# Keeping the w_out result in PSUM for its norm, moving the per-layer products, and eight conditioning columns beside w_out

## The chip, the cores and the metric

The kernel runs on one core of a Trainium2 chip. The metric is the device time of one execution in microseconds, taken as the median of several runs of the same program. A core has five engines that run side by side: TensorE (matrix products, PE in the profile, its weight loads PEld), VectorE (DVE), ScalarE (ACT), GpSimd (POOL) and SyncE (SP), whose queue issues nearly all loads. Each engine works through its own instructions in order, and waits on semaphores for the others.

## What is computed

The input is one sequence of 256 positions with 1024 channels. Two blocks follow each other. The first one is, cut to what matters here:

```
mix = concat(rwkv7(z_rw), nsa(z_nsa), s5(z_s5)) @ w_out      # z = rms_norm(h) @ w_in
h = h + rms_norm(mix, post_mix_norm)
f = conv_ffn(rms_norm(h, pre_ffn_norm), w_up, conv_w, conv_b, w_down)
h = h + rms_norm(f, post_ffn_norm)
e = rms_norm(p @ w_ple, ple_norm)                            # the per-layer vector
h = h + sigmoid(h @ w_ple_gate) * e
```

The second block has a pooling mixer, a feed-forward layer, dilated attention, and a last feed-forward layer. Each of its norms is modulated by columns of `silu(c) @ ada_w + ada_b`: 112 columns of 128 channels, each the product of a 1024-long vector with 128 rows of a matrix. Everything is float32 to the accuracy of the reference.

## The kernel before, in words

The sequence stays transposed on the chip: `xT` is 8 tiles of 128 channels by 256 positions. A weight comes as a 512 KB load on SP's queue into a `raw` tile; ScalarE casts it to a rounded part `wr` (L213), VectorE subtracts to get the remainder `wl` (L214), the input is split in the same way into `R` and `L` (L281 and L282, or L284 and L285 with modulation), and each 128 x 128 step is three matrix products: `R` by `wr` (L224), `L` by `wr` (L225), `R` by `wl` (L226). All other products go through one helper (L241).

A norm works as follows. ScalarE squares each of 8 tiles (L249), TensorE sums the squares over channels with a vector of ones (L241, `st<-ones,sq`), VectorE makes mean plus epsilon (`rv`, L269), GpSimd takes the power -1/2 (`rr`, L271), TensorE spreads the factors over all partitions (`st<-cst,rr`), and VectorE multiplies.

The order of each engine's instructions comes from a scheduler that simulates the program as it is written; `high_priority`, `issue_after`, `behind` (a floor under the simulated start of a piece) and `manual_schedule` (an order written by hand for one engine) change it. It is fixed when the program is built.

The stage that the change touches first is the end of the mixers. `products` runs the w_out steps for eight output tiles, held in two PSUM tiles of tag `acc` and two of tag `ms`. Beside them the tail of the RWKV mixer runs: L720 centres the heads, L721 and L722 square and scale them on ScalarE, L1093 sums, L737 takes the power, L1117 spreads it, L742 and L743 finish, and a split feeds the last w_out steps. L756 then copies each result tile, scaled by the norm's gain, into the SBUF tile `F`, and L249 squares it. `post_add` multiplies `F` by the factors (L1248), adds it to `xT` (L1250), and squares and sums the new `xT` for the norm ahead of the feed-forward layer. Then `ada_setup` loads c into `cond` and takes its silu (L1194, L1195), `ada_rows(ROWS[0])` computes one group of four conditioning columns on TensorE (`acc<-adw,ccol`), `norm_split` makes the feed-forward input (L296, L281, L282), `ple_vec` makes the per-layer vector from `pT` and two `w_ple` loads (L1365 and a sum over squares that GpSimd adds in pairs, L253), and `ffn_up` starts.

The conditioning columns come in two ways: singly on VectorE (`ada`, a load and L1208, a multiplication with sum), or in groups of four on TensorE, `ROWS` of them at five places: (1, 2, 0, 0, 2). The last place is the end of the second block's first feed-forward layer, right before `attention_layer`. There, `norm_split` runs twice on the same factors, into `R`, `L` for the queries and into `raw_x` for keys and values; `bt` tiles (L1524) hold the distances scaled by the heads' slopes.

## Time and profile before

| | |
|---|---|
| median of 3 runs | 1255.55 us (1253.08 to 1264.51) |
| the profiled execution | 1257.43 us |
| its span on the core | 1255.6 us |
| mean granted TensorE clock | 0.967 of full speed |

All rows further down come from the profiled execution; times in them count from the start of its span. "Idle before" in a row, in brackets, is how long the engine stood and what ended it. A matmul's own duration is longer than the distance to the next one, since matmuls are pipelined; where a price per row is wanted, the distance of starts counts. The granted clock is 1.00 at 2.4 GHz and 0.50 at 1.2 GHz.

### The profile page before, as it was taken

How to read it: one execution, taken by the hardware profiler on the slowest of the kernel's cores; microseconds unless marked ns; L12 is line 12 of the kernel's file. 1: busy time of each engine (PE TensorE's matmuls, PEld its weight loads, DVE VectorE, ACT ScalarE, POOL GpSimd, SP SyncE). 2: the span in 40 equal slices, each digit the busy share in tenths (PEclk: the TensorE clock that was granted, in tenths of full speed). 3: DMA queues.
4: the chain of work that ended last, by engine and by line, in shares of the span. 5: the costliest groups of instructions: out<-in, count | busy, mean ns of one | idle time of the engine just before them, and what ended most of it. 6: DMA issues, size and time to landing. Idle time of an engine off the chain costs nothing. (4 is left out here: it accounts for less than half of the span.)

```text
span 1255.6 us, 26442 instructions
## 1 busy us (share of the span) xinstructions
PE 1184.4 (94%) x10664; PEld 1116.8 (89%) x10664; DVE 934.8 (74%) x1839; ACT 680.5 (54%) x1197; POOL 95.8 (8%) x121
## 2 busy tenths in 40 slices
PE   5998999899999998899999988999999999999996
PEld 5985777899999988889999987999999989999996
DVE  7899856389999767979998756756675756987653
ACT  7632644366665535556565445545655565666541
POOL 0022200020000102220000010000000002000010
PEclk9998989799999988999999997999999999999998
DMA  8521302377667873666887785665464624666651
GB/s 286 159 87 51 103 27 77 123 255 252 236 235 261 316 272 112 230 205 250 285 301 249 265 296 192 225 218 201 169 217 168 211 93 153 220 250 219 184 185 34
DMA packets 75707, 247.19 MB, mean 197 GB/s; under 512 B 8256, under 2 KB 15680, under 8 KB 75584
## 3 DMA queue, kind: packets, MB, share of 16 engines
q1 hardware_dynamic: 75296, 244.72, 55.8%
q8 instruction: 83, 1.36, 0.4%
q10 hardware_dynamic: 288, 0.79, 0.2%
q14 instruction: 40, 0.33, 0.1%
HBM read 244.42 MB, written 1.05 MB: 195 GB/s over the span
## 5 line engine op out<-in xcount | busy, mean ns | idle before, releaser
L214 DVE TENSOR_TENSOR wl<-raw,wr 128x1024 fp32r<-128x1024 f32 (+3 forms) x340 | 400.8, 1182 | 128.8 <-ACT wr L213 128.0
L213 ACT CAST wr<-raw 128x1024 fp32r<-128x1024 f32 (+3 forms) x340 | 343.0, 1014 | 266.1 <-PE acc L225 210.8
L224 PE MATMUL acc<-R,wr 128*128 128x256 f32 x1424 | 400.2, 282 | 5.5 <-ACT wr L213 5.2
L226 PE MATMUL acc<-R,wl 128*128 128x256 f32 x1424 | 399.9, 281 | 3.9 <-DVE wl L214 3.7
L225 PE MATMUL acc<-L,wr 128*128 128x256 f32 x1424 | 399.5, 281 | 0.0
L224 PEld LDWEIGHTS acc<-R,wr 128*128 128x128 f32 x1424 | 270.3, 190 | 9.8 <-ACT wr L213 5.5
L226 PEld LDWEIGHTS acc<-R,wl 128*128 128x128 f32 x1424 | 271.2, 191 | 7.6 <-DVE wl L214 5.0
L225 PEld LDWEIGHTS acc<-L,wr 128*128 128x128 f32 x1424 | 270.3, 190 | 1.8 <-issue 1.5
L224 PE MATMUL acc<-aR,wr 128*128 128x256 f32 x608 | 168.7, 281 | 7.2 <-ACT aR L281 6.4
L226 PE MATMUL acc<-aR,wl 128*128 128x256 f32 x608 | 169.0, 280 | 2.4 <-DVE wl L214 2.4
L225 PE MATMUL acc<-aL,wr 128*128 128x256 f32 x608 | 168.6, 279 | 0.1
L1208 DVE SCALAR_TENSOR_TENSOR adw<-adw,cond 128x1024 f32<-128x1024 f32 x92 | 113.0, 1232 | 43.9 <-DMA adw<-in_ada_dram 43.5
L224 PEld LDWEIGHTS acc<-aR,wr 128*128 128x128 f32 x608 | 115.1, 191 | 7.8 <-ACT aR L281 6.8
L226 PEld LDWEIGHTS acc<-aR,wl 128*128 128x128 f32 x608 | 115.3, 190 | 3.7 <-DVE wl L214 3.7
L225 PEld LDWEIGHTS acc<-aL,wr 128*128 128x128 f32 x608 | 115.2, 190 | 0.5 <-DVE aL L282 0.3
L253 POOL TENSOR_TENSOR sq<-sq,sq 128x256 f32<-128x256 f32 x42 | 46.4, 1104 | 867.3 <-ACT sq L249 702.2
L224 PE MATMUL acc<-raw_x,wr 128*128 128x256 f32 (+1 forms) x320 | 92.1, 288 | 1.4 <-ACT wr L213 1.1
L225 PE MATMUL acc<-raw_x,wr 128*128 128x256 f32 (+1 forms) x320 | 91.5, 286 | 1.4 <-DVE raw_x L318 1.3
L226 PE MATMUL acc<-raw_x,wl 128*128 128x256 f32 (+1 forms) x320 | 91.6, 287 | 0.8 <-DVE wl L214 0.8
L241 PE MATMUL acc<-wr,raw_x 128*128 128x256 f32 x384 | 69.0, 281 | 0.0
L225 PEld LDWEIGHTS acc<-raw_x,wr 128*128 128x128 f32 x320 | 61.6, 193 | 2.6 <-DVE raw_x L318 2.1
L226 PEld LDWEIGHTS acc<-raw_x,wl 128*128 128x128 f32 x320 | 61.3, 192 | 2.3 <-issue 1.4
(473 smaller groups left out, 1805.8 us busy)
## 6 DMA issues: line engine op xcount, KB each, us to landing
adw<-in_ada_dram SPq DMA_DIRECT2D x92, 512.0 KB, 5.6
raw<-in_ffn_w_up_dram SPq DMA_DIRECT2D x88, 512.0 KB, 4.3
raw<-in_w_up_dram SPq DMA_DIRECT2D x44, 512.0 KB, 3.3
raw<-in_ffn_w_down_dram SPq DMA_DIRECT2D x32, 512.0 KB, 4.1
raw<-in_attn_w_q_dram SPq DMA_DIRECT2D x24, 512.0 KB, 5.7
raw<-in_w_k_dram SPq DMA_DIRECT2D x24, 512.0 KB, 3.4
raw<-in_w_v_dram SPq DMA_DIRECT2D x24, 512.0 KB, 4.1
adw<-in_ada_r_dram SPq DMA_DIRECT2D x20, 512.0 KB, 5.9
```

Of the source, the lines that this page charges most:

```text
L213: nc.scalar.copy(wr, raw)
L214: nc.vector.tensor_sub(wl, raw, wr[:].bitcast(F32))
L224: mm(out, wr, xr, start=start, stop=False)
L225: mm(out, wr, xl, start=False, stop=False)
L226: self.last_mm = mm(out, wl, xr, start=False, stop=stop).ins
L241: self.nc.tensor.matmul(out, lhsT, rhs, start=start, stop=stop)
L253: nc.gpsimd.tensor_tensor(sq, sq, self.sqsum, op=ALU.add)
L1208: nc.vector.scalar_tensor_tensor(w, w, 1.0, self.cond, op0=ALU.mult, op1=ALU.mult, accum_out=self.mod[:, i:i + 1])
```

## The change

The result tiles of w_out stay in their PSUM tiles. A new `mix_add` takes the factors into SBUF (`keep_r`, `rbq`) and multiplies straight from PSUM, gain and factors in one instruction, before it adds to `xT`. `ple_vec` becomes three parts: its loads and its eight products now stand in `mix_add`, its sums and factors inside the first feed-forward step. In the mixers a second silu(c), `KC`, is made, and eight single columns (`MIXC`) are multiplied on VectorE beside w_out, from loads in the mixers' `raw` buffers. The row groups on TensorE go from (1, 2, 0, 0, 2) to (0, 2, 0, 0, 1). Weight casts and remainders made ahead get floors, and so do the `bt` copies and the silu of `cond`. PSUM pools are closed by hand so that the mixers' tiles live on.

```diff
 UPA = 1
+
+MIXC = 8
 MSB = 3
 ADRB = 6
-ROWS = (1,2,0,0,2)
+ROWS = (0,2,0,0,1)
 ZSB = 2
...
         self.since += 1
-        with self.behind(self.hold if self.hold and self.since > NH else self.floor):
+        hold = self.hold if self.hold and self.since > NH else None
+        with self.behind(hold or self.floor[:1]):
             nc.scalar.copy(wr, raw)
+        with self.behind(hold or self.floor):
             nc.vector.tensor_sub(wl, raw, wr[:].bitcast(F32))
...
         sq = self.tmp([128, T], "sq", bufs=3)
-        nc.scalar.activation(sq, x, AF.Square)
+        self.last_sq = nc.scalar.activation(sq, x, AF.Square).ins
         first = n - 2 if pre else 0
         if pre and k < n - 1:
             if k:
                 nc.gpsimd.tensor_tensor(sq, sq, self.sqsum, op=ALU.add)
             self.sqsum = sq
-        def sums():
+        def sums(st=st):
             for h in range(2):
                 self.mm(st[:, h:h + 1], sq[:, h * 128:(h + 1) * 128], self.ones1,
                         start=(k == first and h == 0), stop=(k == n - 1 and h == 1))
-        if later and k == n - 1:
+        if later and k > n - 1 - later and k >= first:
             return sums
...
             v = self.tmp([128, 2], "rv")
-            nc.vector.tensor_scalar(v, st, 1.0 / D, EPS, op0=ALU.mult, op1=ALU.add)
+            self.last_rv = nc.vector.tensor_scalar(v, st, 1.0 / D, EPS, op0=ALU.mult, op1=ALU.add).ins
             r = self.tmp([128, 2], "rr") if r is None else r
...
                     nc.vector.tensor_tensor(Oc[:, j], Oc[:, j], bon[:, j], op=ALU.add)
-                    self.split(Oc[:, j], self.R[:, j], self.L[:, j])
+                    done = self.split(Oc[:, j], self.R[:, j], self.L[:, j])
             k5 = [weights(4 * i, 4, 5, 1) for i in range(2)]
         for w in k4 + k5:
             early(w, self.last_bc)
+        cond = self.mxt([128, D], "KC")
+        nc.sync.dma_start(cond, self.a["c"].to_broadcast([128, D]))
+        nc.scalar.activation(cond, cond, AF.Silu)
+        for i in self.ada_todo[:MIXC]:
+            w = self.rawload(self.a["ada"][i], [128, D])
+            with self.behind(done):
+                nc.vector.scalar_tensor_tensor(w, w, 1.0, cond, op0=ALU.mult, op1=ALU.mult, accum_out=self.mod[:, i:i + 1])
+        nc.vector.tensor_tensor(self.mod[:, 0:MIXC], self.mod[:, 0:MIXC], self.vcol("ada_b_2", 0, MIXC), op=ALU.add)
+        self.ada_todo = self.ada_todo[MIXC:]
         self.dump("o_rw", Oc)
-        F = self.mxt([128, KB, T], "z9")
         st = self.psum("st", 1)
         for m in range(KB):
             if m % 2 == 0:
                 products(c[m // 2], m)
                 products(c[m // 2], m + 1)
-            nc.scalar.activation(F[:, m], out(m), AF.Identity, scale=self.vcol("post_mix_norm", m))
             self.sq_stat(st, out(m), m, pre=False)
-        return self.post_add(F, self.rstd(st[:, 0:2]), True)
+        self.mix_z = out
+        return st
+
+    def mix_add(self, st):
+
+        nc, tc = self.nc, self.tc
+        load, tile, end = self.ple_vec()
+        load()
+        self.keep_r(self.rstd(st[:, 0:2]))
+        sx = self.psum("ms", MSB)
+        with tc.manual_schedule(engines={mybir.EngineType.DVE}):
+            for k in range(KB):
+                y = self.tmp([128, T], "ny", bufs=3)
+                nc.vector.scalar_tensor_tensor(y, self.mix_z(k), self.vcol("post_mix_norm", k), self.rbq, op0=ALU.mult, op1=ALU.mult)
+                x = nc.vector.tensor_tensor(self.xT[:, k], self.xT[:, k], y, op=ALU.add)
+                self.sq_stat(sx, self.xT[:, k], k, pre=False)
+        rb = self.rstd(sx[:, 0:2])
+        self.floor = self.last_sq, self.last_rv
+        for m in range(KB):
+            tile(m)
+        return rb, end
     def nsa_cmp(self):
...
         nc.sync.dma_start(self.cond, a["c"].to_broadcast([128, D]))
-        nc.scalar.activation(self.cond, self.cond, AF.Silu)
+        with self.behind():
+            nc.scalar.activation(self.cond, self.cond, AF.Silu)
     def ada(self, n):
...
         self.ada_rows(ROWS[1])
-        self.post_add(F, self.rstd(st[:, 0:2]), False)
-
-    def post_add(self, F, rb, stat):
+        self.post_add(F, self.rstd(st[:, 0:2]))
+
+    def post_add(self, F, rb):
         nc = self.nc
-        st = self.psum("acc", self.nacc) if stat else None
         with self.tc.manual_schedule(engines={mybir.EngineType.DVE}):
             for k in range(KB + 1):
                 if k < KB:
                     nc.vector.tensor_tensor(F[:, k], F[:, k], rb, op=ALU.mult)
-                if stat and k < KB:
+                if k:
+                    hold = self.split(self.xT[:, k - 1], self.R[:, k - 1], self.L[:, k - 1])
+                if k < KB:
                     nc.vector.tensor_tensor(self.xT[:, k], self.xT[:, k], F[:, k], op=ALU.add)
-                    self.sq_stat(st, self.xT[:, k], k, pre=False)
-                elif not stat:
-                    if k:
-                        hold = self.split(self.xT[:, k - 1], self.R[:, k - 1], self.L[:, k - 1])
-                    if k < KB:
-                        nc.vector.tensor_tensor(self.xT[:, k], self.xT[:, k], F[:, k], op=ALU.add)
-        if not stat:
-            self.keep_free(hold)
-        return st
+        self.keep_free(hold)
     def addg(self, W, R, L, g, kb, hook=None, perm=False, ahead=False):
...
         pT = self.fp.tile([128, 2, T], F32, name="pT", tag="pT", bufs=1)
-        nc.scalar.dma_start(pT, a["p"].rearrange("p (k t) -> p k t", k=2))
-        st = self.psum("st", 1)
-        for c in range(2):
-            w = self.rawload(a["w_ple"][c].rearrange("p (m k f) -> p m k f", m=4, k=2), [128, 4, 2, 128])
-            for i in range(4):
-                m = 4 * c + i
-                pz = self.psum("acc", self.nacc)
-                for k in range(2):
-                    self.mm(pz[:, 0:T], w[:, i, k], pT[:, k], start=(k == 0), stop=(k == 1))
-                nc.scalar.activation(E[:, m], pz[:, 0:T], AF.Identity, scale=self.vcol("ple_norm", m))
-                self.sq_stat(st, pz[:, 0:T], m)
-        rb = self.rstd(st[:, 0:2])
-        for m in range(KB):
-            nc.vector.tensor_tensor(E[:, m], E[:, m], rb, op=ALU.mult)
+        w, st, pz = [], [], []
+
+        def load():
+            nc.sync.dma_start(pT, a["p"].rearrange("p (k t) -> p k t", k=2))
+            for c in range(2):
+                w.append(self.rawload(a["w_ple"][c].rearrange("p (m k f) -> p m k f", m=4, k=2), [128, 4, 2, 128]))
+
+        def tile(m):
+            if m % 2 == 0:
+                pz.append(self.psum("mx" if m < 4 else "acc", 2))
+                for i in range(2):
+                    for k in range(2):
+                        self.mm(pz[-1][:, i * T:(i + 1) * T], w[m // 4][:, m % 4 + i, k], pT[:, k], start=(k == 0), stop=(k == 1))
+            z = pz[-1][:, m % 2 * T:(m % 2 + 1) * T]
+            nc.scalar.activation(E[:, m], z, AF.Identity, scale=self.vcol("ple_norm", m))
+            sums = self.sq_stat(None, z, m, later=2)
+            if sums:
+                st.append(sums)
+
+        def end():
+            s = self.psum("acc", self.nacc)
+            for sums in st:
+                sums(s)
+            rb = self.rstd(s[:, 0:2])
+            for m in range(KB):
+                nc.vector.tensor_tensor(E[:, m], E[:, m], rb, op=ALU.mult)
+        return load, tile, end
     def ple_gate(self, hook):
...
             for r, c in enumerate((slice(0, 256), slice(256, 384), slice(384, 512))):
-                nc.scalar.activation(b_[:, :, c], self.dt[:, :, c], AF.Copy, scale=8.0 * float(DIL_SLOPES[r, 2 * m + hf]))
+                with self.behind():
+                    nc.scalar.activation(b_[:, :, c], self.dt[:, :, c], AF.Copy, scale=8.0 * float(DIL_SLOPES[r, 2 * m + hf]))
             bt.append(b_)
...
     psum = lambda name: tc.tile_pool(name=name, bufs=1, space=PSUM, reuse_waits="tile")
-    with tc.tile_pool(name="wpm", bufs=1, reuse_waits="tile") as n.wp, psum("psm") as n.ps:
+    mixp, ffp = ExitStack(), ExitStack()
+    n.ps = mixp.enter_context(psum("psm"))
+    n.mixp = mixp
+    with tc.tile_pool(name="wpm", bufs=1, reuse_waits="tile") as n.wp:
         n.nraw, n.nw, n.nacc = RAWM, WM, 2
         n.setup()
         st = n.first()
-        n.dump("x1", n.xT)
-        rb = n.rstd(st[:, 0:2])
     n.wp = ctx.enter_context(tc.tile_pool(name="wp", bufs=1, reuse_waits="tile"))
     n.nraw, n.nw, n.nacc = RAWB, WB, ACCB
     rt = ctx.enter_context(tc.tile_pool(name="rt", bufs=1, reuse_waits="tile"))
     n.skip(rt, SKIP_R)
     n.rawt = rt.tile([128, KB, 2, T + 64], F32R, name="raw_x")
     n.cdp = ctx.enter_context(tc.tile_pool(name="cdp", bufs=1, reuse_waits="tile"))
-    with tc.tile_pool(name="fp", bufs=1, reuse_waits="tile") as n.fp, psum("psf") as n.ps:
+    with tc.tile_pool(name="fp", bufs=1, reuse_waits="tile") as n.fp:
         n.tp = n.fp
-        n.ada_setup()
-        n.ada_rows(ROWS[0])
         n.aR = n.fp.tile([128, FT, T], F32R, name="aR")
         n.aL = n.fp.tile([128, FT, T], F32R, name="aL")
+        rb, end = n.mix_add(st)
         n.norm_split(n.xT, rb, n.vcol("pre_ffn_norm", 0, 8), n.R, n.L)
-        n.ple_vec()
-        n.ffn_up(a["w_up"], lambda m: n.ada(ADA[1]), True, "conv_w", "conv_b")
+        n.ada_setup()
+        mixp.close()
+        n.ps = ffp.enter_context(psum("psf"))
+        n.ffn_up(a["w_up"], lambda m: n.ada(ADA[1]) if m else end(), True, "conv_w", "conv_b")
         n.post(a["w_down"], n.aR, n.aL, n.vcol("post_ffn_norm", 0, 8), FT, lambda m: n.ada(ADA[2]))
         n.second_ahead()
         st = n.ple_gate(lambda m: n.ada(ADA[7]))
         n.dump("x2", n.xT)
         if upto >= 5:
             rb = n.second(*st)
+    ffp.close()
     if upto >= 6:
```

Three places of the order follow; first come the rows before, then those of the changed kernel.

ScalarE at the tail of the RWKV mixer (`KC` is the second copy of c, `mx` the heads from L720, whose line is now L725; L721 and L722 are now L726 and L727):

```order
L904 COPY z_380_2228<-ms_2468 128x512
L721 ACTIVATE sq_446_2541<-mx_2542 128x256
L722 ACTIVATE t_445_2540<-mx_2542,vec 128x256
L721 ACTIVATE sq_446_2541<-mx_2546 128x256
L722 ACTIVATE t_445_2540<-mx_2546,vec 128x256
L918 COPY z_380_2228<-st_2401 128x256
L281 CAST R<-z_380_2228 128x256
L721 ACTIVATE sq_446_2541<-mx_2550 128x256
L722 ACTIVATE t_445_2540<-mx_2550,vec 128x256
```

```order
L936 COPY z_380_2228<-ms_2468 128x512
L755 ACT_TABLE_LOAD
L755 ACTIVATE KC_2740<-KC_2740 128x1024
L726 ACTIVATE sq_446_2541<-mx_2542 128x256
L727 ACTIVATE t_445_2540<-mx_2542,vec 128x256
L726 ACTIVATE sq_446_2541<-mx_2546 128x256
L727 ACTIVATE t_445_2540<-mx_2546,vec 128x256
L950 COPY z_380_2228<-st_2401 128x256
L285 CAST R<-z_380_2228 128x256
L726 ACTIVATE sq_446_2541<-mx_2550 128x256
L727 ACTIVATE t_445_2540<-mx_2550,vec 128x256
```

A table load and the silu of `KC` stand where nothing stood, ahead of all six squares and copies of the tail.

TensorE between the last sums of w_out and the first feed-forward product (`sq` with `ones` are sums of squares, `pT` with `raw` the per-layer products, `adw` a row group):

```order
L241 MATMUL st_2741<-ones_86,sq_2850 128x1 x2
L241 MATMUL st_2858<-cst,rr_2856 128x128 x2
L241 MATMUL acc_2861<-ones_86,sq_2866 128x1 x2
...
L241 MATMUL acc_2861<-ones_86,sq_2908 128x1 x2
L241 MATMUL st_2919<-cst,rr_2917 128x128 x2
L241 MATMUL acc_2944<-adw_2946,ccol 32x128 x8
...
L241 MATMUL acc_2944<-adw_2966,ccol 32x128 x8
L241 MATMUL acc_3032<-pT,raw_3030 128x256 x2
L241 MATMUL acc_3038<-pT,raw_3030 128x256 x2
...
L241 MATMUL acc_3084<-pT,raw_3059 128x256 x2
L224 MATMUL acc_3107<-R,wr_3110 128x256
```

```order
L245 MATMUL st_2768<-ones_86,sq_2869 128x1 x2
L245 MATMUL st_2902<-cst,rr_2900 128x128 x2
L245 MATMUL mx_2973<-pT,raw_2894 128x256 x4
L245 MATMUL mx_2985<-pT,raw_2894 128x256 x4
L245 MATMUL acc_2998<-pT,raw_2896 128x256 x4
L245 MATMUL ms_2906<-ones_86,sq_2912 128x1 x2
...
L245 MATMUL ms_2906<-ones_86,sq_2926 128x1 x2
L245 MATMUL acc_3011<-pT,raw_2896 128x256 x4
L245 MATMUL ms_2906<-ones_86,sq_2933 128x1 x2
...
L245 MATMUL ms_2906<-ones_86,sq_2961 128x1 x2
L245 MATMUL st_2970<-cst,rr_2968 128x128 x2
L228 MATMUL acc_3066<-R,wr_3069 128x256
```

The row group is gone, and the per-layer products moved from behind the second norm's factors to a place ahead of and between its sums.

ScalarE at the entry to the attention layer (`row` is the copy that a row group needs, `R` and `raw_x` the two splits, `QK` the copy of queries and keys):

```order
L249 ACTIVATE sq_9282<-xT 128x256
L1524 ACTIVATE bt_10064<-dt 128x2x256
...
L1524 ACTIVATE bt_10561<-dt 128x2x128 x2
L284 ACTIVATE R<-ny_9400,mod 128x256
L284 ACTIVATE R<-ny_9402,mod 128x256
L1145 COPY row_9287<-acc_9286 128x128
L284 ACTIVATE R<-ny_9406,mod 128x256
...
L284 ACTIVATE raw_x<-ny_9461,mod 128x256
L213 CAST wr_9600<-raw_9598 128x1024
L213 CAST wr_9630<-raw_9628 128x1024
L1493 COPY QK_9472<-acc_9473 128x512
```

```order
L253 ACTIVATE sq_9257<-xT 128x256
L288 ACTIVATE R<-ny_9334,mod 128x256
...
L288 ACTIVATE R<-ny_9344,mod 128x256
L1177 COPY row_9262<-acc_9261 128x128
L288 ACTIVATE R<-ny_9348,mod 128x256
...
L288 ACTIVATE raw_x<-ny_9395,mod 128x256
L216 CAST wr_9534<-raw_9532 128x1024
L1564 ACTIVATE bt_9998<-dt 128x2x256
...
L1564 ACTIVATE bt_10495<-dt 128x2x128 x2
L216 CAST wr_9564<-raw_9562 128x1024
L1532 COPY QK_9406<-acc_9407 128x512
```

The nine `bt` copies moved from ahead of the first split to behind the second one and a first cast, ahead of the next cast and of the first `QK` copy; one `row` copy is gone.

## Rows read from the trace of the kernel before

**Rows 1.** The page's first and fifth part: busy time and instructions; groups by line.

```profile
PE 1184.4 (94%) x10664; PEld 1116.8 (89%) x10664; DVE 934.8 (74%) x1839; ACT 680.5 (54%) x1197; POOL 95.8 (8%) x121
...
L214 DVE TENSOR_TENSOR wl<-raw,wr 128x1024 fp32r<-128x1024 f32 (+3 forms) x340 | 400.8, 1182 | 128.8 <-ACT wr L213 128.0
L213 ACT CAST wr<-raw 128x1024 fp32r<-128x1024 f32 (+3 forms) x340 | 343.0, 1014 | 266.1 <-PE acc L225 210.8
...
L1208 DVE SCALAR_TENSOR_TENSOR adw<-adw,cond 128x1024 f32<-128x1024 f32 x92 | 113.0, 1232 | 43.9 <-DMA adw<-in_ada_dram 43.5
```

**Rows 2.** Windows: length, busy PE, PEld, DVE, ACT, POOL (instructions), clock, DMA, GB/s.

```profile
200.00:220.00 20.00, 20.00 (x182) 16.98 (x179) 10.09 (x20) 8.80 (x18) 2.98 (x3) 1.00 0.28 93
...
254.00:256.00 2.00, 2.00 (x10) 1.73 (x9) 1.96 (x6) 1.15 (x4) 0.00 (x0) 0.91 0.70 250
...
749.00:753.00 4.00, 0.73 (x5) 0.52 (x4) 1.24 (x4) 2.31 (x7) 0.71 (x1) 0.96 0.96 338
...
764.00:770.00 6.00, 5.74 (x28) 5.66 (x29) 5.57 (x16) 3.24 (x7) 0.00 (x0) 0.52 0.01 3
770.00:778.00 8.00, 8.00 (x73) 8.00 (x72) 5.01 (x7) 4.25 (x6) 0.00 (x0) 1.00 0.40 118
```

**Rows 3.** Time line of SP's queue, 190 to 250: start, us to issue, instruction.

```profile
204.39 0.50 SPq L1194 DMA_DIRECT2D cond<-in_c_dram  x1
```

**Rows 4.** DMA issues of 200 to 275: count, KB each, median us to landing.

```profile
cond<-in_c_dram SPq DMA_DIRECT2D x1, 512.0 KB, 4.4
```

**Rows 5.** Time line of ScalarE, 196 to 275: start, us, instruction, idle before.

```profile
204.44 0.38 ACT L721 ACTIVATE sq<-mx 128x256 f32<-128x256 f32 x1 [1.68 <-PE mx L720]
...
246.45 1.28 ACT L1195 ACT_TABLE_LOAD   x1
247.75 1.06 ACT L1195 ACTIVATE cond<-cond 128x1024 f32<-128x1024 f32 x1
```

**Rows 6.** Groups by line, 200 to 275: count, busy us, mean ns, idle before.

```profile
L296 DVE SCALAR_TENSOR_TENSOR ny<-xT,vec,st 128x256 f32<-128x256 f32 x8 | 3.7, 476 | 2.1 <-PE st L241 2.1
...
L1250 DVE TENSOR_TENSOR xT<-xT,z 128x256 f32<-128x256 f32 x8 | 3.4, 425 | 0.3
...
L1248 DVE TENSOR_TENSOR z<-z,st 128x256 f32<-128x256 f32 x8 | 3.3, 416 | 2.2 <-PE st L241 2.2
...
L756 ACT ACTIVATE z<-acc,vec 128x256 f32<-128x256 f32 x4 | 1.9, 475 | 6.1 <-PE acc L226 6.1
```

**Rows 7.** Time line of TensorE, 204 to 214.

```profile
207.90 0.59 PE L720 MATMUL mx<-t,csm 128*128 128x256 f32 x2
```

**Rows 8.** Time line of VectorE, 234 to 275.

```profile
237.16 0.16 DVE L269 TENSOR_SCALAR rv<-st 128x2 f32<-128x2 f32 x1 [13.98 <-PE st L241]
...
247.97 0.16 DVE L269 TENSOR_SCALAR rv<-acc 128x2 f32<-128x2 f32 x1 [1.80 <-PE acc L241]
```

**Rows 9.** Time line of TensorE, 234 to 275.

```profile
240.95 6.99 PE L241 MATMUL acc<-ones,sq 128*128 128x1 f32 x32 [1.57 <-ACT sq L249]
...
250.11 2.79 PE L241 MATMUL acc<-adw,ccol 128*32 128x128 f32 x48
252.83 7.92 PE L241 MATMUL acc<-pT,raw 128*128 128x256 f32 x32
...
263.28 0.64 PE L241 MATMUL acc<-adw,ccol 128*32 128x128 f32 x16
...
267.06 0.38 PE L241 MATMUL st<-ones,sq 128*128 128x1 f32 x2 [0.56 <-POOL sq L253]
```

**Rows 10.** Time line of TensorE, 738 to 766.

```profile
755.60 2.21 PE L241 MATMUL acc<-adw,ccol 128*32 128x128 f32 x32 [4.67 <-DMA adw<-in_ada_r_dram]
...
764.40 0.58 PE L224 MATMUL acc<-R,wr 128*128 128x256 f32 x1 [0.26 <-DVE mod L1149]
```

**Rows 11.** Time line of ScalarE, 742 to 792.

```profile
750.69 3.50 ACT L1524 ACTIVATE bt<-dt 128x512 f32<-128x512 f32 x9 [2.33 <-DMA dt<-in_dist_dram]
...
770.49 0.51 ACT L284 ACTIVATE raw_x<-ny,mod 128x256 fp32r<-128x256 f32 x1 [0.28 <-DVE ny L296]
```

More of the change, by code (lines that the diff above doesn't have):

```diff
@@ L374, in mixers @@
         tc, a = self.tc, self.a
-        with tc.tile_pool(name="mx", bufs=1, reuse_waits="tile") as mx, tc.tile_pool(name="mxp", bufs=2, space=PSUM, reuse_waits="tile") as self.px:
+        with tc.tile_pool(name="mx", bufs=1, reuse_waits="tile") as mx:
+            self.px = self.mixp.enter_context(tc.tile_pool(name="mxp", bufs=2, space=PSUM, reuse_waits="tile"))
             self.mx = self.tp = mx
```

## The prediction

> **What bounds the kernel now.** I read the page's busy table first: TensorE is busy 94% of the span, no other engine above 74% [rows 1]. So time is to be won only where TensorE stops, and I went on to the windows. In the stretch before the end of the w_out products TensorE has no idle slice (20.00 of 20 us), and neither has it once attention runs (8.00 of 8 us from 770) [rows 2]. There, work that TensorE needs later than planned moves the end one for one, and work on other engines that comes earlier gains nothing. The reader should see two holes that the change touches. The first is the pair of norms after w_out, from the last product's sums to the feed-forward products, where VectorE's adds limit and TensorE's clock is low: it is back at 2.4 GHz only within the window from 254 to 256 (0.91 granted) [rows 2]. The second is the entry to the attention layer, where TensorE is busy 0.73 of the 4 us from 749 [rows 2]. Last I read the order of the instructions, since the change moves many of them, and the time line of each engine round the places that moved.
>
> **Term 1: the new copy of c on ScalarE, +4.0 us.** The eight columns need silu(c) in a second tile. Its load stands in SP's queue where before the load of `cond` stood, right behind the last w_out loads: issued at 204.39 [rows 3], landing 4.4 us later [rows 4], so at 208.8. The order shows that the table load and the Silu stand ahead of the squares and copies of the RWKV tail (L721, L722) in ScalarE's order, and the table load holds the wait for this DMA. Before, these began at 204.44 [rows 5]. Now: 208.8 + 1.28 table load + 1.06 Silu [rows 5] = 211.1, plus the first square, 0.38 [rows 5], and the scaled copy behind it, as long as L756's 0.47 [rows 6], less 0.1 by which they overlap (estimate), = 211.9. TensorE's third L720 product needs the PSUM buffer that this copy frees; it ran at 207.90 [rows 7]. TensorE then waits 4.0 us, and everything behind it in that stage (head sums, normalised heads, the last w_out products) waits with it, with no slack [rows 2]. Bounds: nothing, if the wait is hidden in a way that I don't see (rival A), and 2 more if the clock falls in the wait (rival B). The load's row is that of the same source at the same place in the queue, so I take its 4.4.
>
> **Term 2: the end of w_out, -0.5.** Eight scaled copies of the result (L756, 0.47 each [rows 6]) leave ScalarE. All but the last pair lay beside products; after the last product the second square comes one copy earlier, so the first `rv`, 237.16 [rows 8], comes 0.5 earlier. The eight columns cost VectorE 8 x 1.23 = 9.9 us (L1208 [rows 1]) and SP eight 512 KB loads. Their cover is VectorE's 13.98 us without work ahead of `rv` [rows 8] and a DMA share of 0.28 [rows 2]. The loads go through four buffers, so pairs of products are spaced by landings; I put the last product's end at 240, just ahead of the later `rv`: cost nothing, 0.5 at worst.
>
> **Term 3: addition and second norm, +5.6 against before.** First `rv` is now 237.16 - 0.5 + 4.0 = 240.7. The factors take 2.3 as before (0.16 of `rv` [rows 8] and the 2.2 that VectorE then waits ahead of L1248 [rows 6]), and copying them out of PSUM 0.45, estimated by the copies of that size (L756): first add at 243.5. A pair was a 416 ns product and a 425 ns addition; the product becomes a scalar_tensor_tensor, 476 ns by L296 [rows 6]: +0.06 x 8 = +0.5. The operand now comes from PSUM instead of SBUF; the row of L1248, which reads the factors there, is as short as that of L1250, which does not [rows 6], so I add nothing for it. The Trainium skill, page "Perfetto Trace Analysis", section "Optimizing Scalar/DVE Operations", gives VectorE about 125 ns of access overhead on PSUM against 60 on SBUF; by it the eight products would cost another 0.5 and the sum below would be -0.7 instead of -1.2; the two rows here do not show that difference. The additions thus end at 250.4.
> But "beside its addition" is not what TensorE's order says: 24 of the 32 rows of the per-layer products stand ahead of the second norm's first sums, the other 8 ahead of its fourth. The first w_ple load waits for the eighth column's product (its buffer), about 240, and I give it the 4.4 us of the load of `cond` [rows 4]: 244. The 32 rows took 7.92 us, of which the first ran at the low clock [rows 9]: 0.42 us each there, 0.21 at 2.4 GHz. The clock came back at about 254.3 (0.91 of 254 to 256), 4.2 us after TensorE became busy at 250.11 [rows 2, 9]; I take the same here: 10 rows low, 22 high, 4.2 + 4.6 = 8.8, then 32 sum rows at 0.125 (by the clock about half of the 0.22 that they took low, 6.99 us for 32 [rows 9]) = 4.0 more. The second `rv` falls at 257, where before it was at 247.97 [rows 8]: 9 later, 4.0 of it term 1. Given back: the row group of four columns (48 rows, 2.79 us [rows 9]) and the products are gone from behind. Behind `rv`, VectorE first takes three weight remainders (L214, 1.18 each [rows 1]), which it did later before; the factors are ready inside this time, and the split of eight tiles at 0.73 to 0.8 each follows (one L296 of 476 ns [rows 6] and one remainder); with a little for Pool's adds, which some of its casts stand behind, I get the first feed-forward chain's end at 268.3. It was at 263.28 [rows 9]: 5.0 later. Later in that stage, row products (0.64), a wait for Pool (0.56) [rows 9] and the rows' transposition (by two rows of that kind 0.4, estimate) are gone: -1.6. So terms 1 to 3 give +3.4 together (4.0 - 0.6). Bounds: 5.7 less if w_ple lands early enough that the additions limit (251.3), 2 more if the clock comes back only at the sums.
>
> **Term 4: entry to the attention layer, -4.6.** One of two row groups goes. Before, the first attention product at 764.40 waited for the second group's columns (its row names `mod`, L1149 [rows 10]). Nine `bt` copies (3.50 us from 750.69 [rows 11]) ran ahead of the first split on ScalarE and now stand behind both splits. The one group left needs its fourth load, used at 755.60 before [rows 10]; so its rows end at 756.7, its columns near 757.7, where the chains start, paced by the split. A ninth column now sits in VectorE's order between the third and fourth remainder and waits for a load issued one place behind: some 1.5 us. The second split waited for the same `mod` and ran from 764.4 to 771.0 [rows 10, 11]; now it would run from 760.2 to 766.8. New wait: behind it ScalarE does one weight cast (1.0, L213 [rows 1]), the nine `bt` copies (3.5 [rows 11]), another cast and the copy of Q and K (0.6, estimate: an L756 of twice the width), which frees the bank for the fifth chain: 772.9. Before, that chain began at 777.6: 764.40, then 96 rows, 23 of them at 0.21 until 769.3 and 73 at 0.11 (28 rows in 6 us, 73 in 8) [rows 2, 10]. Gain 4.6 to 4.7, I take 4.6; bounds 3 (the clock low once more in the new wait) and 6.5 (the wait hidden).
>
> **Sum.** +3.4 - 4.6 = -1.2 on the profiled 1257.43 us: 1256.2. That execution lies 1.88 above the median of the runs; against 1255.55 the sum gives **1254.4**.
>
> **Rivals.** A: the copy of c costs nothing: its load comes well ahead of the tail, so TensorE's hole at 207.9 is absent: 1254.4 - 4.0 = 1250.4. For it: TensorE reaches the third L720 3.5 us later than ScalarE its first square [rows 5, 7], so a load 4 us earlier would do. Against: SP's time and the 4.4 us [rows 3, 4]. With it, the additions as the limit (-5.7) and the best of term 4 (-1.9) the end would be 1242.8, the only way that I see to over 1%.
> B, slower than before: the clock falls in the 4.0 us hole at 208. [...] The products behind then run 4.2 us at 1.2 GHz, which costs 2.1 in a stage without slack: 1256.5. The Trainium skill, page "TensorE: Matmul & The Clock Gate", section "What's actually happening", has the clock set by how busy the engine has recently been; the trace agrees at 749.
> C, slower as well: term 4 brings nothing. The ninth column's load or the `bt` copies hold the fifth chain until 777.6 (its point: the second split must end later than 771, as before). Then +3.4: 1259.0; with B 1261.1. For it: ScalarE's 6.1 us of work that now stands on that path. Against: second split starts 4 us earlier on every row that I have.
> D: the change does not do what it says. In part so above; if w_ple lands later still, each us costs one: 1256 to 1259, inside C's time.
>
> **Numbers.** Forecast 0.40 (1252 to 1256), A 0.20, B 0.17, C with D 0.18, unseen 0.05. A to C with their bounds span 1247 to 1262: predicted 1254.4, range 1247 to 1262. The runs of before spread from 1253.08 to 1264.51, so about 1% (12.6 us) is what can be told from no change. Faster by that needs A and every best bound: 0.12, from A's 0.20; slower needs C, B and the worst of terms 1 and 3 (+2 each): 0.06, from C's. Within: 0.82.
>
> **What would show it.** Term 1: the Silu on ScalarE ending near 211 and TensorE idle for some 4 us before its third L725 product; if it is idle under 1 us, A. Granted clock below 1.00 between 208 and 220 means B. Term 3: second `rv` near 257, and per-layer products ahead of the sums at the low clock; a second `rv` before 253 would make it wrong. Term 4: the first attention chain some 6 us earlier against the end of the last feed-forward product, then ScalarE's `bt` copies with TensorE waiting behind them. No hole there, or a hole of over 6 us, makes the term wrong.

## The result, and the profile after

The changed kernel took 1266.37 us (median of 20 runs, 1259.84 to 1275.89), the kernel before, run beside it, 1260.99 (20 runs, 1250.67 to 1271.50): a ratio of 1.0061, 95% interval 1.0039 to 1.0083. In a second comparison the ratio was 1.0017 (0.9987 to 1.0047). By the ratios the change costs 8 and 2 us, by the medians 5.4 and 0.2 (the second pair is 1264.92 against 1264.70); the second comparison can't be told from no cost. I forecast a gain of 1.2, and 1266.4 lies outside my range. Of the 12.0 us between 1254.4 and 1266.37, 5.4 are the base (the three runs that I built on had a median of 1255.55, the 20 runs one of 1260.99) and 6.6 the change: the 5.4 that it cost, and the 1.2 that I had it gain.

The profiled execution of after took 1275.89 us (span 1274.1), the slowest of its 20; that of before had 1257.43. Of these 18.5 us, 7.5 lie between two executions of the kernel before alone, as the control shows below. Busy times on the page hardly moved (row 1 of [rows 1]):

```profile
PE 1195.6 (94%) x10532; PEld 1131.1 (89%) x10532; DVE 946.4 (74%) x1854; ACT 677.8 (53%) x1189; POOL 90.9 (7%) x121
```

**The tail ahead of w_out's end.** ScalarE's time line of after, which answers to [rows 5], with start, length, instruction and idle time ahead:

```profile
208.04 1.28 ACT L755 ACT_TABLE_LOAD   x1 [6.30 <-DMA KC<-in_c_dram]
209.34 1.06 ACT L755 ACTIVATE KC<-KC 128x1024 f32<-128x1024 f32 x1
...
210.57 0.47 ACT L727 ACTIVATE t<-mx,vec 128x256 f32<-128x256 f32 x1
```

TensorE's time line, answering to [rows 7] and, further on, to [rows 9]:

```profile
211.09 1.22 PE L725 MATMUL mx<-t,csm 128*128 128x256 f32 x2 [3.93 <-ACT t L727]
...
245.88 4.77 PE L245 MATMUL mx<-pT,raw 128*128 128x256 f32 x16
250.49 1.89 PE L245 MATMUL acc<-pT,raw 128*128 128x256 f32 x8
252.21 1.40 PE L245 MATMUL ms<-ones,sq 128*128 128x1 f32 x12
253.47 1.97 PE L245 MATMUL acc<-pT,raw 128*128 128x256 f32 x8
255.28 2.29 PE L245 MATMUL ms<-ones,sq 128*128 128x1 f32 x20
...
265.23 0.58 PE L228 MATMUL acc<-R,wr 128*128 128x256 f32 x1 [4.48 <-ACT sq L253]
```

The windows of after (columns as in [rows 2]; the ninth number is the granted clock):

```profile
205.00:215.00 10.00, 6.07 (x35) 5.31 (x36) 1.39 (x2) 5.01 (x10) 0.00 (x0) 0.78 0.14 54
215.00:225.00 10.00, 10.00 (x83) 9.11 (x82) 3.86 (x8) 3.21 (x5) 3.39 (x5) 0.88 0.32 107
```

Here the reader sees ScalarE held 6.3 us by a table load that waits for a DMA, TensorE idle for 3.93 us behind it, and then what the forecast did not have: a clock that falls to 1.2 GHz for a part of the next 20 us, in a stretch that before, up to 220, had 1.00 and no idle time [rows 2]. VectorE's two `rv`, to be set against [rows 8]:

```profile
243.88 0.16 DVE L273 TENSOR_SCALAR rv<-st 128x2 f32<-128x2 f32 x1 [0.77 <-PE st L245]
...
257.61 0.16 DVE L273 TENSOR_SCALAR rv<-ms 128x2 f32<-128x2 f32 x1 [4.15 <-PE ms L245]
```

**The entry to the attention layer.** TensorE and then ScalarE of after, answering to [rows 10, 11]:

```profile
769.43 1.08 PE L245 MATMUL acc<-adw,ccol 128*32 128x128 f32 x16 [5.13 <-DMA adw<-in_ada_r_dram]
...
771.35 0.56 PE L228 MATMUL acc<-R,wr 128*128 128x256 f32 x1
...
787.14 0.39 PE L228 MATMUL acc<-raw_x,wr 128*128 128x256 f32 x1 [1.90 <-ACT QK L1532]
```

```profile
780.81 0.51 ACT L288 ACTIVATE raw_x<-ny,mod 128x256 fp32r<-128x256 f32 x1 [0.28 <-DVE ny L300]
781.22 1.04 ACT L216 CAST wr<-raw 128x1024 fp32r<-128x1024 f32 x1
782.16 3.51 ACT L1564 ACTIVATE bt<-dt 128x512 f32<-128x512 f32 x9
785.58 1.03 ACT L216 CAST wr<-raw 128x1024 fp32r<-128x1024 f32 x1
786.51 0.57 ACT L1532 COPY QK<-acc 128x512 f32<-128x512 f32 x1
```

The windows of that stretch of after:

```profile
786.00:790.00 4.00, 2.86 (x14) 2.87 (x15) 3.16 (x3) 3.46 (x5) 0.00 (x0) 0.68 0.31 94
790.00:794.00 4.00, 4.00 (x34) 4.00 (x33) 1.67 (x3) 1.05 (x1) 0.00 (x0) 0.89 0.97 333
```

The wait for the `bt` copies is as forecast, and behind it the clock is low once more (0.68, 0.89).

### The profile page after: what moved, and what is told of

Its sections match the earlier page's. It is cut to its first block, busy times and chain, and to the rows that moved or that the text cites. A ratio compares the mean times of both kernels' runs of the same rounds, so it can differ in the third digit from the quotient of the medians.

```text
span 1274.1 us, 26203 instructions
## 1 busy us (share of the span) xinstructions
PE 1195.6 (94%) x10532; PEld 1131.1 (89%) x10532; DVE 946.4 (74%) x1854; ACT 677.8 (53%) x1189; POOL 90.9 (7%) x121
## 3 DMA queue, kind: packets, MB, share of 16 engines
HBM read 244.95 MB, written 1.05 MB: 193 GB/s over the span
## 5 line engine op out<-in xcount | busy, mean ns | idle before, releaser
L228 PE MATMUL acc<-R,wr 128*128 128x256 f32 x1424 | 405.3, 285 | 9.1 <-ACT wr L216 4.7
L230 PE MATMUL acc<-R,wl 128*128 128x256 f32 x1424 | 405.7, 285 | 3.6 <-DVE wl L218 3.4
L229 PE MATMUL acc<-L,wr 128*128 128x256 f32 x1424 | 404.0, 284 | 0.0
L228 PEld LDWEIGHTS acc<-R,wr 128*128 128x128 f32 x1424 | 275.8, 194 | 13.9 <-ACT wr L216 4.9
L257 POOL TENSOR_TENSOR sq<-sq,sq 128x256 f32<-128x256 f32 x42 | 42.3, 1007 | 873.5 <-ACT sq L253 853.3
L228 PE MATMUL acc<-raw_x,wr 128*128 128x256 f32 (+1 forms) x320 | 94.0, 294 | 3.4 <-ACT QK L1532 1.9
L229 PE MATMUL acc<-raw_x,wr 128*128 128x256 f32 (+1 forms) x320 | 93.5, 292 | 1.8 <-DVE raw_x L322 1.7
L228 PEld LDWEIGHTS acc<-raw_x,wr 128*128 128x128 f32 x320 | 63.3, 198 | 4.5 <-ACT QK L1532 2.1
L229 PEld LDWEIGHTS acc<-raw_x,wr 128*128 128x128 f32 x320 | 63.4, 198 | 3.4 <-DVE raw_x L322 2.9
```

The lines of the kernel that those rows point to most:

```text
L228: mm(out, wr, xr, start=start, stop=False)
L229: mm(out, wr, xl, start=False, stop=False)
L230: self.last_mm = mm(out, wl, xr, start=False, stop=stop).ins
L257: nc.gpsimd.tensor_tensor(sq, sq, self.sqsum, op=ALU.add)
```

## The experiments

For each kernel I read four points from its trace: the first `rv` behind w_out; the start of the 200th feed-forward product; the time from the `rv` ahead of the attention layer (749.22 in before) to that layer's 160th product of R or L with a weight ("entry"); and the span. Products are counted from 0. "Wide" counts neighbouring 256-column products of TensorE that start 117 to 119 ns apart; the others start 113 or 114 apart. A ratio is against the kernel before timed beside that kernel (20 to 29 runs); the kernels had 12 runs each, after 20, e_all2 6, c_before and e_bt0 one.

| kernel | first rv | 200th | entry | wide | span | ratio to before (95%) |
|---|---|---|---|---|---|---|
| before | 237.2 | 287.1 | 75.2 | 2384 | 1255.6 | |
| c_before, the same | 237.2 | 287.2 | 73.5 | 5405 | 1263.1 | |
| after | 243.9 | 295.6 | 73.5 | 5643 | 1274.1 | 1.0061 (1.0039-1.0083) |
| c_after, the same | 242.7 | 293.1 | 73.8 | 4221 | 1269.3 | 1.0017 (0.9987-1.0047) |
| e_silu | 237.5 | 287.4 | 73.7 | 4362 | 1258.3 | 0.9962 (0.9933-0.9992) |
| e_ple | 242.3 | 289.0 | 70.8 | 2769 | 1253.5 | 0.9969 (0.9938-0.9999) |
| e_silu_ple | 235.4 | 281.5 | 71.2 | 2732 | 1246.7 | 0.9969 (0.9943-0.9994) |
| e_bt0 | 243.9 | 294.5 | 72.7 | 2624 | 1264.2 | one run |
| e_bt1 | 242.1 | 292.3 | 72.0 | 4390 | 1267.0 | 1.0060 (1.0031-1.0089) |
| e_col | 244.6 | 296.0 | 69.5 | 1113 | 1257.8 | 1.0019 (0.9995-1.0043) |
| e_all | 235.3 | 281.7 | 70.2 | 2720 | 1247.4 | 0.9977 (0.9952-1.0002) |
| e_all2 | 236.0 | 282.6 | 69.3 | 4151 | 1249.5 | 0.9918 (0.9888-0.9949) |

**Controls: each kernel once more (c_before, c_after).** No edit.

> The kernel before, once more, for a second profile. In the first profile most back-to-back 256-column products of TensorE started 113 to 114 ns apart, in the changed kernel's most started 117 to 119 ns apart, both at a granted clock of 1.00. Theory L (the spacing is drawn per execution and stall, whatever the program): this profile may show any mix, and its span lies 0.0042 us per wide-spaced product away from the other's, so up to some 20 us apart. Theory P (the spacing belongs to the program): about 4750 narrow and 2380 wide pairs again, and a span within 3 us of 1255.6.

> The changed kernel, once more, for a second profile and a second ratio. Theory L: the share of wide-spaced products differs from the first profile's (1462 narrow, 5643 wide), the stalls do not: third L725 some 4 us late with the clock low behind it, second rv near 257, fifth attention chain behind the bt copies; ratio again 1.004 to 1.008. Theory P: mostly wide again, span within 3 us of 1274.1.

Theory L holds, but not in its price. The second profile of the same kernel before has more than twice the wide pairs and is 7.5 us longer, 2.5 ns for each further wide pair where I expected 4.2. Three windows of before's first execution, and then of its second; the first count is TensorE's products in 50 us:

```profile
300.00:350.00 50.00, 50.00 (x426) 50.00 (x426) 46.69 (x87) 32.66 (x54) 0.00 (x0) 1.00 0.63 224
610.00:660.00 50.00, 50.00 (x444) 50.00 (x443) 46.51 (x87) 29.32 (x49) 0.00 (x0) 1.00 0.82 286
1090.00:1140.00 50.00, 50.00 (x444) 50.00 (x443) 43.53 (x79) 32.42 (x53) 0.00 (x0) 1.00 0.71 254
```

```profile
300.00:350.00 50.00, 50.00 (x427) 50.00 (x426) 47.41 (x88) 33.27 (x56) 0.00 (x0) 1.00 0.66 233
610.00:660.00 50.00, 50.00 (x427) 50.00 (x426) 44.74 (x84) 27.92 (x45) 0.00 (x0) 1.00 0.80 278
1090.00:1140.00 50.00, 50.00 (x427) 50.00 (x427) 43.51 (x76) 30.86 (x52) 0.00 (x0) 1.00 0.71 251
```

TensorE is busy without a gap and granted its full clock in all six, yet in the second and third window it does 444 products in the one execution and 427 in the other; in the first both executions have the wide spacing. So spans of single profiles can't be compared here; points inside stages of equal spacing can (up to the 1000th feed-forward product, near 380, both executions of before agree within 0.1 us). Against c_before, whose spacing is nearest to after's, after is 11.0 us longer: 6.7 at the first `rv`, 1.7 more by the 200th feed-forward product, 2.1 more by the `rv` ahead of attention, 0.1 less over the entry, 0.6 in the rest. The second profile of after, c_after, shows the same stalls (4.03 us ahead of the third L725 product, 2.05 ahead of the fifth chain) and is 6.2 us longer than c_before, 5.5 of it at the first `rv` and 0.5 more by the 200th product. Both profiled executions of the changed kernel lie above the median of its runs, by 9.5 and 6.2 us, so single profiles show more loss than the medians do; and c_after's ratio, 1.0017, is below the 1.004 to 1.008 that I expected.

**Silu of KC behind the tail (e_silu).**

```
-        nc.scalar.activation(cond, cond, AF.Silu)
+        with self.behind(done): nc.scalar.activation(cond, cond, AF.Silu)
```

> The changed kernel with the table load and Silu of KC placed behind the RWKV tail on ScalarE. Theory M (the wait for KC's load is what costs): TensorE's third L725 without a wait of over 1 us, granted clock 1.00 over 205 to 225, everything behind it 4.2 us (the hole) + 2.1 us (the low clock) earlier, the first rv near 237.5; time 5 to 6 us below the changed kernel's, ratio to before 1.000 to 1.002. Rival E (the eight columns' loads and products set the first rv, 243.9, whatever ScalarE does): first rv stays within 2 us, time within 2 us of the changed kernel's. Theory P would see no change that is not in the spacing.

Theory M holds for the time, and rival E falls as I put it, though its mechanism is there (below). TensorE's and ScalarE's time lines of e_silu:

```profile
206.75 0.59 PE L725 MATMUL mx<-t,csm 128*128 128x256 f32 x2
```

```profile
220.38 1.28 ACT L755 ACT_TABLE_LOAD   x1
221.68 1.06 ACT L755 ACTIVATE KC<-KC 128x1024 f32<-128x1024 f32 x1
```

and its windows:

```profile
205.00:215.00 10.00, 10.00 (x88) 9.34 (x86) 3.38 (x5) 3.82 (x7) 3.08 (x5) 1.00 0.39 134
215.00:225.00 10.00, 9.86 (x90) 8.90 (x89) 7.07 (x14) 4.08 (x6) 0.00 (x0) 1.00 0.30 111
```

The hole and the low clock are gone together, the first `rv` is 6.3 us earlier than in after (5.2 against c_after), 0.3 to 0.4 behind where it was before the change, with all eight columns still there. The time fell by 5.1 us against c_after, timed beside it (1259.86 and 1264.92); the ratio, 0.9962, is lower than the 1.000 to 1.002 that I expected.

The columns are not out of the way, though. VectorE's eighth column product and then ScalarE, in after:

```profile
241.17 1.23 DVE L759 SCALAR_TENSOR_TENSOR raw<-raw,KC 128x1024 f32<-128x1024 f32 x1 [1.41 <-DMA raw<-in_ada_dram]
```

```profile
242.70 0.20 ACT L314 CAST raw_x<-mod 128x16 fp32r<-128x16 f32 x1 [1.29 <-DVE cws L1316]
242.81 0.38 ACT L253 ACTIVATE sq<-ms 128x256 f32<-128x256 f32 x1
```

A small cast of the columns (L314) stands ahead of the last square of w_out in ScalarE's order and waits until VectorE is through with the eighth product. In all ten profiles of changed kernels the first `rv` starts 1.48 us behind that product's end, and TensorE stands 0.2 to 1.8 us ahead of the last sums (1.08 in after, 1.76 in e_silu), where before it did not stand. The columns' products start behind the tail, so they came earlier with it. No run leaves them out, so what they cost is not measured.

**Per-layer products behind the second norm's sums (e_ple), and both edits (e_silu_ple).**

```
-        rb = self.rstd(sx[:, 0:2])
+        sums, rb = self.mm_ins, self.rstd(sx[:, 0:2])
         ...
         for m in range(KB):
-            tile(m)
+            with self.behind((sums,)): tile(m)
```

(`mm_ins` is the last matrix product that was written, here the last of the sums.)

> The changed kernel with the 32 per-layer products placed behind the second norm's sums on TensorE, so that they fill the wait for its factors. Theory M3 (the products ahead of the sums make the second rv late): second rv at the end of the additions, near 254.5 instead of 257.6; the products then run beside Pool's power and VectorE's split, first feed-forward product 2 to 3 us earlier; time 2 to 3 us below the changed kernel's. Rival S (the split is held by VectorE's weight remainders, ScalarE's order and Pool's adds): rv early, but the first feed-forward product within 1 us, time unchanged; or the broadcast of the factors falls behind products at 0.3 us each and it gains nothing.

> Silu of KC behind the RWKV tail and per-layer products behind the second norm's sums, with the bt copies where the change put them. Theory A1 (the two edits of the first region carry the gain): feed-forward products 5 us ahead of the kernel before, as with all three edits, and from the ninth rv to the 160th attention product 73.5 us as in the changed kernel, against 70.3 with all three; ratio to before 0.997 to 0.999, some 2 us above that of the three. Theory A2 (the bt edit matters): 4 us or more above.

M3 holds. The second `rv`, at 252.99, is 1.5 us earlier than expected, the first feed-forward product at 263.13 comes 2.1 and 1.5 us earlier than in after and c_after, and the time is 3.6 us below c_after's (1261.36 and 1264.92), a little more than I expected. In e_ple the second `rv` comes 10.7 us behind the first, where it was 13.7 and 14.3 in the two executions of after and 10.8 before. TensorE's time line of e_ple:

```profile
245.93 7.02 PE L245 MATMUL ms<-ones,sq 128*128 128x1 f32 x32 [1.95 <-ACT sq L253]
252.81 6.36 PE L245 MATMUL mx<-pT,raw 128*128 128x256 f32 x16
259.01 1.46 PE L245 MATMUL acc<-pT,raw 128*128 128x256 f32 x6
```

TensorE is busy while Pool raises to the power, so the clock is back before the feed-forward begins; in after it is low over its first products. The windows in which the first product falls, of e_ple and of after:

```profile
260.00:265.00 5.00, 4.60 (x25) 3.55 (x23) 2.97 (x7) 4.21 (x14) 3.65 (x5) 1.00 0.97 370
```

```profile
265.00:270.00 5.00, 4.77 (x28) 4.77 (x28) 4.38 (x12) 3.95 (x11) 2.23 (x3) 0.64 0.57 220
```

From the first `rv` to the 200th product it takes 46.7 us, against 50.4 and 51.7 in the two of after and 49.9 before: 3.7 to 5.0 us less than in after. Both edits put that product at 281.5, 5.6 ahead of c_before (some 0.4 of it by the narrow spacing that e_silu_ple has there; e_all, with the wide one, has 281.7), and A1 holds for this region. The ratio is the expected one, if not above that of the three edits (e_all). What I expected of the entry (73.5) missed: 71.2. With the placement of the `bt` copies unchanged, e_ple and e_silu_ple pass the entry 2 to 3 us faster than after, c_after and e_silu; their clock does not fall a second time there, though TensorE waits longer for the `QK` copy than the 1.90 us of after: 2.35 in e_ple (until 774.95, with a granted clock of 1.00 from 775 to 780) and 2.28 in e_silu_ple. So the length of a wait alone does not tell whether the clock falls behind it; what decides was not tested.

**The `bt` copies ahead of the first split (e_bt0) or behind the first QK copies (e_bt1).** For e_bt1:

```
-                with self.behind():
+                with self.behind((self.qk_ins[m],) if m < 2 else None):
                     nc.scalar.activation(b_[:, :, c], ..., AF.Copy, ...)
```

(`qk_ins` holds the copies of Q and K.) In e_bt0 the floor is empty, `self.behind(())`.

> The changed kernel with the bt copies free to stand ahead of the first split on ScalarE, as before. Theory Q: the first attention product comes 3.5 us later against the end of the feed-forward than in the changed kernel, the fifth chain no later; so of the 6 us some 2.5 are left at the entry and the same 2.5 are left 40 products on: nothing is given back there. Rival W: later by 3.5 at both places.

> The changed kernel with the bt copies of the first two pairs of heads placed behind the copy of that pair's Q and K on ScalarE, not ahead of it. Matched product by product with the kernel before, the changed kernel enters the attention layer 6 us better than it left the feed-forward, and 6 us worse again some 40 products later. Theory Q (the nine bt copies ahead of the first QK copy hold the PSUM bank of the fifth chain, and the clock falls in that wait): the 2 us wait before that chain goes, no clock below 1.00 from 786 to 791, and 4 to 6 us of the gain stay; time 4 to 6 us below the changed kernel's. Rival W (the late second split or the weight casts hold the chains): the same 5 to 6 us are lost with the bt copies out of the way, time within 2 us of the changed kernel's.

Theory Q holds by half. The 2 us wait ahead of the fifth chain is gone in both, and the next hundred products lose nothing. But e_bt1's time is no better than after's (1.0060, where I expected 4 to 6 us less), and its entry only 1.5 to 1.8 us shorter: a second wait stands behind the first. TensorE of e_bt1:

```profile
792.96 0.51 PE L245 MATMUL acc<-wr,raw_x 128*128 128x256 f32 x2 [2.18 <-DVE V L1551]
```

and its VectorE:

```profile
786.56 1.23 DVE L1241 SCALAR_TENSOR_TENSOR adw<-adw,cond 128x1024 f32<-128x1024 f32 x1 [5.54 <-DMA adw<-in_ada_dram]
...
791.21 1.22 DVE L218 TENSOR_TENSOR wl<-raw,wr 128x1024 fp32r<-128x1024 f32 x1
...
792.49 0.42 DVE L1551 COPY V<-acc 128x256 f32<-128x256 f32 x1
```

VectorE stands 5.54 us at a column whose load has not landed; weight remainders and the V copy that frees TensorE's bank stand behind it in order. For e_bt0 I expected the first attention product 3.5 us later than in after; it came 7.9 us behind the `rv`, 0.9 earlier than there, since ScalarE makes the copies (761.97 to 765.47) while TensorE waits anyway, and 0.8 to 1.1 us were kept instead of 2.5.

**The first three columns later (e_col).** On top of e_bt1:

```
-                    self.ada(ADA[6])
+                    self.ada((0, 4, 4, 4)[2 * hg + i] if hg < 2 else ADA[6])
```

> The kernel with the bt copies behind the QK copy, and with the first three columns of the attention layer handed to the next three pairs of heads, so that the first pair's V copies on VectorE no longer stand behind loads of columns. Theory D (after the bt wait goes, VectorE's 5.5 us wait for a column's load is next, and holds the V copies and weight remainders): TensorE's 2.2 us wait for a V copy near 793 and the low clock behind it go; from the ninth rv to the 160th attention product 68 to 69 us, where the bt edit alone has 72.0, the changed kernel 73.5 to 73.8, the kernel before 73.6 to 75.2. Rival W2 (the weight loads themselves set the pace, at some 400 GB/s): VectorE then waits for weights, and it stays at 71 to 73.

Theory D holds: the entry takes 69.5 us (expected 68 to 69), against 72.0 in e_bt1 and 73.5 in c_before. A window of e_bt1 with the hole, and then e_col's, without a hole and at full clock:

```profile
790.00:794.00 4.00, 1.82 (x14) 1.63 (x14) 4.00 (x10) 1.45 (x2) 0.00 (x0) 0.95 0.55 164
```

```profile
785.00:793.00 8.00, 8.00 (x69) 7.54 (x68) 3.64 (x5) 5.92 (x10) 0.00 (x0) 1.00 0.58 203
793.00:800.00 7.00, 7.00 (x63) 6.75 (x62) 4.35 (x11) 3.72 (x6) 0.00 (x0) 1.00 0.91 313
```

**Three edits (e_all), all four (e_all2).**

> The three edits together: Silu of KC behind the RWKV tail, the per-layer products behind the second norm's sums, the bt copies behind the QK copy. If each loss is one of its own place they add: first rv at 237.5, second at 248 to 249, feed-forward products 2 to 4 us ahead of the kernel before, attention 6 to 9 us ahead of it; median 0.6 to 0.9% below the kernel before. If the places overlap (the clock's fall behind the norms is paid anyway, or the weight casts are next), it stays within 2 us of the best single edit, a ratio of 0.996.

> All four edits: Silu behind the tail, products behind the sums, bt copies behind the QK copy, the first three columns later. Theory D: some 3 us below the version with three edits, ratio to before 0.994 to 0.996. W2: as with three edits, 0.997 to 0.998.

At its points e_all is better than expected (235.3; 5.5 ahead of c_before at the 200th product; 9.9 ahead of c_before at the 560th attention product), but its median was only 0.2% below that of before: less than the 0.6 to 0.9% that I expected, and not to be told from e_silu_ple. With the columns later as well, e_all2 is furthest below the kernel before: 0.9918 (0.9888 to 0.9949), 1249.15 us (6 runs) against 1258.94 (23). That is more than the 0.994 to 0.996 that I expected, and the last edit explains only a part: timed beside e_silu_ple, e_all2 is 5.3 us faster, of which its entry has 1.9; against e_all, timed in another comparison, it is some 7 us faster by the two ratios, of which its entry has 0.9. Where the rest comes from was not found.

## Why the prediction was wrong, step by step

**Term 1 held in mechanism, and its consequence was mis-chosen.** I forecast the scaled copy's end at 211.9 and a wait of 4.0; the third product began at 211.09 after 3.93 us. But rival B, a clock that falls in that hole, I priced at +2.1 and gave 0.17; it came in all six profiles, of five kernels, that kept the Silu there (first `rv` 242.1 to 244.6, that is +4.9 to +7.4; without it 235.3 to 237.5). The attention entry had shown me a hole with a fall of the clock [rows 2]; a hole of that kind in a stage without slack should have had the fall in the forecast itself. Nor could I tell by the hole's length: in before the clock is also low from 237.3 on (0.81 over 237.0 to 237.5), where TensorE had worked until 237.1, and the 2.35 us wait of e_ple left it at 1.00. Hole and clock went away together, so their shares were not measured apart. By estimate they are 3.9 and 3.2: from 211.0 to 217.5 the granted clock of after is 0.51, and half of those 6.5 us is lost. The twelve sums of w_out ahead of TensorE's last wait there start 7.0 us later in after than in e_silu (240.76 and 233.74), which fits.

**Term 2 came near in size, and its mechanism was wrong.** I forecast -0.5 at the first `rv`, and e_silu has +0.3 to +0.4. I had the eighth column's product end at 240, just ahead of `rv`, and priced it at nothing; it ended at 242.40 in after, and the last square and `rv` stood behind it, as shown with e_silu.

**Term 3 came near in total, by luck.** Second `rv` forecast 257, found at 257.6 and 257.0, though from a later first `rv`: the step between them was 13.7 to 14.3, not 16.3. From there to the 23rd feed-forward product (the place that I called the first chain's end) it took 12.7 and 14.2 us, where I had 11.3, since the clock was low over the first products, which the sum did not have. The two errors nearly cancel: 26.5 and 28.5 from the first `rv`, where I had 27.6. Where I had counted a wait for Pool (0.56) as given back, another one stands in the profiled execution of after (c_after has none), 2.03 us long and with a granted clock of 0.66 over 275 to 280 behind it:

```profile
274.66 0.71 PE L245 MATMUL st<-cst,rr 128*128 128x128 f32 x4 [2.03 <-POOL rr L275]
```

By the 200th product terms 1 to 3 together stood at +5.9 to +8.5, where I had +3.4; in e_silu, without term 1, at +0.2 (I had -0.6 without it), so that most of the excess comes with term 1's hole and clock and what they shift. The product that reads PSUM costs 477 to 479 ns (L783), against 472 of L300, as I assumed. The figures that I quoted from the Trainium skill, page "Perfetto Trace Analysis", section "Optimizing Scalar/DVE Operations", would by estimate make a read from PSUM some 65 ns longer. L300 can't test that, since its factors (`st`) lie in PSUM too, but L1248 with an operand in PSUM and L1250 without, at 416 and 425 ns [rows 6], do not show it. Nor could those 0.5 us have moved my sum, as I let them: I had the additions end 6 us ahead of the second `rv` (at 250.7 by my own terms, not 250.4). Groups by line of after, 200 to 275:

```profile
L300 DVE SCALAR_TENSOR_TENSOR ny<-xT,vec,st 128x256 f32<-128x256 f32 x8 | 3.7, 472 | 0.0
...
L783 DVE SCALAR_TENSOR_TENSOR ny<-ms,vec,rbq 128x256 f32<-128x256 f32 x4 | 1.9, 477 | 0.0
```

**Term 4 failed: -4.6 forecast, +0.3 to -1.8 found, and that is about what two executions of before differ by.** Those differ by 1.7, which the clock accounts for: over the 22 us from the `rv` it was granted at 0.61 in before and 0.69 in c_before. The first half came (8.8 us from `rv` to the first attention product, against 14.6 and 15.2 before: -5.8 or more), and the chain behind the `bt` copies began 24.5 us behind the `rv` (I had 23.7; the 760.2 at which I let the second split begin has no working beside it, and it began 1.3 us later against the `rv`). The step that failed is the end of my path: I stopped the sum at the fifth chain and took what was won there as kept. Counted product by product against c_before, after is 5.8 us ahead at the first attention product, 4.5 ahead eight products before the fifth chain, 2.5 at its start and 0.8 ahead 32 products on: what went there is the wait of 1.90 us and a clock that fell again (0.68 and 0.89 above), which I had only as a bound. With the copies out of the way, the rest is lost further behind (e_bt0, e_bt1), where VectorE's columns and V copies were limited by loads that did not come earlier with the rest. That is rival C with another cause: it was to be decided by the second split, which came early enough (it ended 18.7 us behind the `rv`, 21.8 before). That the gain at the entry is real once both waits are out of the way is shown by e_col.

B with C gave 1261.1 on my base, +5.5 on 1255.55; the measured differences are +5.4 and +0.2. That the first meets it so closely is luck, since C came by another cause than the one that I gave it. I had B at 0.17 and C with D at 0.18 as if only one could come, and did not ask what happens to the range when the base itself moves by 5 us. By the points in the two traces terms 1 to 4 come to some 6 to 8 us, where the medians have 5.4 and 0.2; why the second comparison shows so little stays open.

## What to carry over

A wait in front of an in-order engine was paid twice here where TensorE has no slack: its length, and the low clock behind it; look for the table load or load-bound instruction that stands first in the queue and move it behind the work that is needed. Work that is laid beside other work is free only if nothing that uses it stands ahead of needed work in some engine's order: here a cast of 0.20 us tied the norm to the eighth column. A gain at the entry of a stage is only a gain if the loads behind it come earlier too: follow it to the next instruction that waits for a DMA, on every engine, before it is put into the sum. Where one kernel's runs spread by 1.7%, compare points inside stages, in two profiles of each kernel, not spans.

## What was not expected of the hardware

TensorE has two spacings of 256-column products at the same granted clock of 1.00: 113 to 114 and 117 to 119 ns (444 or 427 products in 50 us). One spacing can hold for hundreds of microseconds, and in every trace it changes many times, at waits or in short irregular stretches; ScalarE's and VectorE's instructions keep their lengths (casts of 1024 columns 1.05 us, remainders 1.22 in either). TensorE's time line of before's first execution goes from the one to the other a few products behind a wait of 0.52 us: what is to be read are the distances of the starts, sixteen in 1.89 us from 403.12 to 405.01, and eight in 0.90 from 406.74 to 407.64:

```profile
403.12 0.28 PE L224 MATMUL acc<-aR,wr 128*128 128x256 f32 x1
...
405.01 0.28 PE L225 MATMUL acc<-aL,wr 128*128 128x256 f32 x1
405.81 0.39 PE L226 MATMUL acc<-aR,wl 128*128 128x256 f32 x1 [0.52 <-DVE wl L214]
...
406.74 0.28 PE L224 MATMUL acc<-aR,wr 128*128 128x256 f32 x1
...
407.64 0.28 PE L226 MATMUL acc<-aR,wl 128*128 128x256 f32 x1
```

The share of wide pairs went from 16% (e_col) to 79% (after). Between the two profiles of before, 3021 more of them went with 7.5 us, 2.5 ns each. What decides which spacing follows a wait was not found, nor whether a program can favour one; that the changed kernel's two profiles had 5643 and 4221, before's 2384 and 5405, is too little to say that the change does.
